# Accumulating weight-sum transfers that wait for the split of the block they follow, four steps per three blocks

## The chip, the cores and the metric

The kernel runs on one core of one Trainium2 chip. The metric is the device time of one execution in microseconds (us), median of three runs. One execution was also recorded by the hardware profiler; its rows are what the prediction argues from.

## What is computed

One layer of an encoder: a token mixer with two groups of recurrent heads, a cross-attention, and a squared-ReLU MLP, each on the RMS-normalised residual stream of 512 tokens by 1024 columns, all in float32. Cut to what matters:

```python
D_MODEL, SEQ, MEM_LEN, D_FF = 1024, 512, 256, 4096
def reference(x, mem, ...):
    x = x + token_mixer(rmsnorm(x, norm_mix[l]), w_in[l], ..., w_out[l])
    x = x + cross_attention(rmsnorm(x, norm_xattn[l]), rmsnorm(mem, norm_mem[l]), w_xq[l], w_xkv[l], w_xo[l])
    x = x + squared_relu_mlp(rmsnorm(x, norm_mlp[l]), w_up[l], w_down[l])
    return rmsnorm(x, norm_final)
def token_mixer(xn, w_in, ...):
    proj = xn @ w_in + b_in                      # q, forget gates, ... of both groups
    hgrn_out  = scan forward + scan backward     # per head, forget gate per key
    mlstm_out = scan forward + scan backward     # per head, running-max stabiliser
    return concatenate([hgrn_out, mlstm_out]) @ w_out
```

## The kernel before

All products run on TensorE as three passes of a fast float32 type: each operand is split into a high and a low part, and `mm3` (L338 to L341) multiplies high by high, high by low and low by high. The split of a weight block, `split_out` (L335, L336), is a copy to `wh` on ScalarE (ACT) and a subtraction to `wl` on VectorE (DVE); both show as L336.

Weights come as 141 blocks of 128 x 1024 (512 KB). The first 75, blocks 0 to 74, are streamed in a fixed order: the mixer's input projection (0 to 36; blocks 5 to 12 belong to the first pair of HGRN heads: q, forward gate, backward gate, output gate), cross-attention's k and v (37 to 52), the mixer's output (53 to 60), cross-attention's q (61 to 68) and the beginning of its output (69 to 74). `weights(key)` (L270) is called as each block's products are written: it splits blocks i to i+2, and has block i+3 loaded by SyncE (SP) (`load`, L251; the transfer is L256, tile `st`, three buffers, and three each of `wh` and `wl`). A load can start when the split of the block three earlier has freed its buffer.

The MLP and part of cross-attention's output use a Strassen-like scheme of seven products P1 to P7 per 2 x 2 blocks, some of which need sums of weight blocks. The DMA engines make these sums in device memory, in tiles named `form_...`: `make_forms` (L297 to L331) yields 88 steps in a fixed order. A *start* copies a block into a form (SP, L293), a *follow* copies a finished form into the next one (SP, L309), and 44 *accumulating steps* add a block into a form that its start or follow has filled (a DMA of GpSimd, POOL, with `accum_op`, L293; the name is `form_P<-in_wpk` at POOL). The first twelve steps are starts. `next_form` (L243) takes the next step: from block 6 on, `weights` calls it once per block, and twice where the block's number is divisible by four, so that 79 steps fall into the streamed blocks; the MLP's `mahead` (L1267) takes the other nine, one at every second block.

A scheduler sets the order of each engine's instructions, and a step's place in it comes from `behind` (L142): an edge without a semaphore that puts the step behind another instruction of the same engine. An SP step is placed behind the last load. An accumulating step is placed behind the last `wl` split, which is VectorE's: across engines such an edge makes nobody wait. So an accumulating step is issued as soon as GpSimd's queue comes to it and the start or follow that it adds to has landed.

GpSimd issues its instructions in order, and has other work: the pow of `rstd_of` (L209), which VectorE's L207 feeds and on which normalisations wait, memsets (`vv` L819, `t` L829 and L830), and loads of the gate and `as` blocks (L1174). `in_turn` (L198) places the pows and some memsets behind all accumulating steps taken so far but the last.

At the place that the prediction speaks of, mixer blocks 8 to 14 are multiplied while VectorE prepares the scans of both groups. Chains of small work are advanced between the blocks. The gate chain of the mLSTM heads loads a mask from memory, `rmask` (128 KB, issued by SP at L761), runs two scans for the running maximum (L775), then two with the mask (L779), then L806, L808 (ScalarE) and L809. The HGRN pair has its gates evacuated with sigmoids (ScalarE L531, L533; VectorE L535, L536) and forms products of the gates level by level (`update`, L549 to L551), which TensorE multiplies at L564. A change of the function on ScalarE brings a table load of its own.

Of the kernel before, what the change touches and what calls it, by code (L numbers as in the profile page):

```python
# [80 lines left out]
def trunk(ctx: ExitStack, tc: tile.TileContext, x, mem, wpk, vec, cst, lmask, rmask, rows, out):  # L81
# [60 lines left out]
    def behind(a, b):  # L142

        tc.add_manual_dep(a.ins, b.ins.name, mybir.DependencyInfo(mybir.DependencyClass.NoSync, mybir.DependencyReason.DATA),
                          reason="order of an engine")

    def load_x(t):
        nc.sync.dma_start(out=xtile[t], in_=x[t * P:t * P + P, :])

    row_load = nc.scalar.dma_start(out=grow1[96:97, :], in_=rows[0:1, :])  # L150
    load_x(0)
    behind(nc.scalar.dma_start(out=cs, in_=cst[:, 0:NC1]), row_load)
    for g in range(2):
# [51 lines left out]
    def rstd_of(ss, w, n):  # L205
        ms = tiny(w)
        v.tensor_scalar(out=ms, in0=ss, scalar1=1.0 / n, scalar2=EPS, op0=ALU.mult, op1=ALU.add)  # L207
        r = tiny(w)
        in_turn(gp.tensor_tensor(out=r, in0=ms, in1=nh.to_broadcast([P, w]), op=ALU.pow))  # L209
        return r, ms  # L210
# [30 lines left out]
    last_load, last_made = [None], [None]  # L241

    def next_form():  # L243

        o = next(form_steps, None)
        if o is not None:
            behind(o, last_load[0] if o.ins.engine == mybir.EngineType.SP else last_made[0])
            if o.ins.engine != mybir.EngineType.SP:
                accs.append(o)


    def load(i):
        if i >= NSTREAM or i in st_tiles:
            return
        t = T("st", 1024, 3)
        last_load[0] = nc.sync.dma_start(out=t, in_=wpk[i])  # L256
        st_tiles[i] = t

    def split(i):
        if i >= NSTREAM or i in hl_tiles:  # L260
            return
        load(i)
        s = st_tiles[i]
        hi, lo = T("wh", 1024, 3, F32R), T("wl", 1024, 3, F32R)
        made = split_out(hi, lo, s)
        last_made[0] = made[1]
        hl_tiles[i] = (hi, lo)
        return made[1]

    def weights(key):  # L270
        i = SIDX[key]
        with (tc.high_priority() if i > 2 else ExitStack()):
            for n in range(i, i + 3):
                split(n)
            load(i + 3)
        for _ in range((i >= 6) + (i >= 6 and i % 4 == 0)):
            next_form()
        return hl_tiles[i]

# [72 lines left out]
    def proj_d(mat, c0, xs, n=512, count=2):  # L352

        for j in range(count):
            wh, wl = weights(("d", mat, 0, c0 + P * j))
            ps = mmb()
            for k in range(8):
                z = slice(k * P, k * P + P)
                mm3(ps[:, :n], wh[:, z], wl[:, z], xs[k][0], xs[k][1], k == 0, k == 7)
                if k == 3:  # L360
                    tick()
            yield ps
            tick()

    def proj_t(mat, k0, c0, xs, ntile=4, pre=None, late=False):

        acc = [mmb() for _ in range(ntile)]

        def part(t, q, w):
            for k in range(2):  # L370
                kk = 2 * q + k
                xh, xl = xs[kk][0][:, t * P:t * P + P], xs[kk][1][:, t * P:t * P + P]
                z = slice(k * 512, k * 512 + 512)
                mm3(acc[t], xh, xl, w[0][:, z], w[1][:, z], kk == 0, kk == 7)

        for q in range(2 if late else 3):
            w = weights(("t", mat, k0 + 2 * q, c0))
            for t in range(ntile):
                part(t, q, w)
                if t % 2 == 1:  # L380
                    tick()
        if pre is not None:
            pre()
        tail = [(q, weights(("t", mat, k0 + 2 * q, c0))) for q in range(2 if late else 3, 4)]
        for t in range(ntile):
            for q, w in tail:
                part(t, q, w)
            yield t, acc[t]
            if t % 2 == 1:
                tick()  # L390
# [3 lines left out]
    xs = xk(xT)  # L394
    load(0)
    load_x(1)
    load(1)
    load_x(2)
    load_x(3)
    load(2)  # L400
# [577 lines left out]
    for t in range(2):  # L978
        a = mt[t]
# [7 lines left out]
        r, _ = rstd_of(ss, 1, D)  # L987
# [279 lines left out]
    def mahead(n):  # L1267
        with tc.high_priority():
            for m in range(n, n + 3):
                msplit(m)  # L1270
            for m in range(n + 3, n + 7):
                mload(m)
        if n % 2 and n >= len(JOBS):
            next_form()
        return mhl[n]
# [468 lines left out]
```

## Time and profile before

| | |
|---|---|
| Median of 3 runs | 834.73 us (832.35 to 836.01) |
| The profiled execution | 835.44 us |
| Its span, first to last instruction | 833.7 us |
| Granted clock of TensorE, mean | 0.992 |
| TensorE (PE) busy | 806.5 us, 97% |
| VectorE (DVE) busy | 618.6 us, 74% |
| ScalarE (ACT) busy | 486.0 us, 58% |
| GpSimd (POOL) busy | 95.1 us, 11% |
| DMA queue q1 (SP's), of 16 engines | 126.04 MB, 42.6% |
| DMA queue q0 (GpSimd's), of 16 engines | 39.85 MB, 26.2% |

A row of the timeline gives start, duration, engine, line, operation, output and inputs, and in brackets the time that the engine stood idle before it with what released it. A row of the chain of waits gives start, duration and what was running in the chain of work that ended last. A row of windows gives a stretch, its length, the busy time and number of instructions of PE, weight loads, DVE, ACT and POOL, then the granted clock (1.00 is full speed), the share of the DMA engines' time in use and GB/s. The numbers L... are lines of the kernel before.

### The profile page before, as it was taken

Reading aid. Unit: us, or ns where it says so; the run is one execution under the profiler, and the core shown is the slowest. Engines: PE = TensorE matmul, PEld = TensorE weight load, DVE = VectorE, ACT = ScalarE, POOL = GpSimd, SP = SyncE. Lnnn points to the kernel's source line nnn. Section 1 sums busy time; section 2 is a strip of 40 time slices with the busy share of each in tenths; the row PEclk is TensorE's granted clock in tenths of the full one; section 3 lists DMA queues with packets and bytes.
Section 4 is the critical chain, followed back from the end, with each engine's and each line's share of the span. In section 5 each row is a group of like instructions: output and inputs, shape, how many; then the busy total and the mean of one; then the engine's idle time right before and its main releaser. Section 6 shows DMA issues by size and latency. Waiting matters only on the chain.

```text
span 833.7 us, 14061 instructions
## 1 busy us (share of the span) xinstructions
PE 806.5 (97%) x5438; PEld 694.7 (83%) x5438; DVE 618.6 (74%) x1033; ACT 486.0 (58%) x854; POOL 95.1 (11%) x130
## 2 busy tenths in 40 slices
PE   8999799999999999999999999999999999999995
PEld 6787588887888988887888889988998899889974
DVE  6566786599568988655567879997479658875885
ACT  5244556444578476454455578874486458546854
POOL 2011000210042020231020012011101000100001
PEclk9999899999999999999999999999999999999998
DMA  7379822397187978997792456679976686768552
GB/s 275 117 208 279 263 92 76 110 241 246 51 229 241 263 203 303 293 222 192 227 214 65 101 127 180 213 192 313 331 236 153 227 278 202 180 203 255 172 151 101
DMA packets 56597, 167.26 MB, mean 201 GB/s; under 512 B 5393, under 2 KB 5521, under 8 KB 56530
## 3 DMA queue, kind: packets, MB, share of 16 engines
q1 hardware_dynamic: 41200, 126.04, 42.6%
q0 software_dynamic: 15040, 39.85, 26.2%
q8 instruction: 43, 0.70, 0.3%
q10 hardware_dynamic: 290, 0.47, 0.2%
q14 instruction: 24, 0.20, 0.1%
HBM read 164.24 MB, written 48.23 MB: 255 GB/s over the span
## 4 chain that ended last, share of the span: by engine, by line
PE 64%; DVE 11%; DMA 9%; issue 8%; ACT 5%; POOL 2%; POOLq 0%; ACTq 0%; SPq 0%; DVEq 0%
PE mm L339 8%; PE mm L341 8%; PE mm L340 8%; DMA st<-in_wpk 5%; PE sm L1300 4%; DVE wl L336 4%; PE sm L1298 4%; PE sm L1299 4%; PE sm L1582 3%; PE sm L1583 3%; PE sm L1581 3%; PE mm L1582 2%; PE mm L1583 2%; PE mm L1581 2%; ACT wh L336 2%
## 5 line engine op out<-in xcount | busy, mean ns | idle before, releaser
L336 DVE TENSOR_TENSOR wl<-st,wh 128x1024 fp32r<-128x1024 f32 x165 | 201.7, 1224 | 106.5 <-ACT wh L336 105.3
L336 ACT ACTIVATE wh<-st 128x1024 fp32r<-128x1024 f32 x165 | 174.2, 1057 | 169.1 <-PE mm L340 44.7
L339 PE MATMUL mm<-xT,wh 128*128 128x512 f32 x288 | 116.3, 405 | 0.0
L341 PE MATMUL mm<-xT,wl 128*128 128x512 f32 x288 | 113.6, 394 | 0.1
L340 PE MATMUL mm<-xT,wh 128*128 128x512 f32 x288 | 113.3, 393 | 0.3 <-DVE xT L1053 0.3
L1300 PE MATMUL sm<-wh,a 128*128 128x512 f32 x180 | 70.5, 392 | 1.5 <-DVE a L336 1.5
L1298 PE MATMUL sm<-wh,a 128*128 128x512 f32 x180 | 70.2, 390 | 0.9 <-DVE vv L1511 0.9
L1299 PE MATMUL sm<-wl,a 128*128 128x512 f32 x180 | 70.1, 389 | 0.0
L341 PEld LDWEIGHTS mm<-xT,wl 128*128 128x128 f32 x288 | 54.3, 189 | 12.0 <-DVE wl L336 0.3
L340 PEld LDWEIGHTS mm<-xT,wh 128*128 128x128 f32 x288 | 54.6, 190 | 11.0 <-DVE xT L1053 0.9
L339 PEld LDWEIGHTS mm<-xT,wh 128*128 128x128 f32 x288 | 54.5, 189 | 11.0 <-ACT wh L336 0.3
L293 POOL DMA_DIRECT2D form_P<-in_wpk x44 | 45.6, 1437 | 95.3 <-DMA form_P<-in_wpk 70.3
L293 POOL DMA_DIRECT2D as<-in_wpk x20 | 17.7, 934 | 255.6 <-DVE wl L336 167.5
L1300 PEld LDWEIGHTS sm<-wh,a 128*128 128x128 f32 x180 | 33.8, 188 | 9.9 <-DVE a L336 3.1
L1298 PEld LDWEIGHTS sm<-wh,a 128*128 128x128 f32 x180 | 33.8, 188 | 8.2 <-ACT wh L336 1.3
L1299 PEld LDWEIGHTS sm<-wl,a 128*128 128x128 f32 x180 | 33.8, 188 | 7.0
L1583 PE MATMUL sm<-yT,wl 128*128 128x256 f32 x128 | 36.4, 285 | 0.8 <-DVE wl L336 0.7
L336 ACT ACTIVATE wh<-as 128x1024 fp32r<-128x1024 f32 x24 | 25.4, 1058 | 20.2 <-PE sm L1300 10.7
L1582 PE MATMUL sm<-yT,wh 128*128 128x256 f32 x128 | 36.3, 284 | 0.7 <-DVE yT L336 0.7
L1582 PE MATMUL sm<-xT,wh 128*128 128x256 f32 x128 | 36.4, 285 | 0.3 <-DVE xT L336 0.2
L1582 PE MATMUL mm<-xT,wh 128*128 128x256 f32 x128 | 36.3, 284 | 0.2 <-DVE xT L336 0.2
L1583 PE MATMUL sm<-xT,wl 128*128 128x256 f32 x128 | 36.4, 285 | 0.0
(388 smaller groups left out, 2121.2 us busy)
## 6 DMA issues: line engine op xcount, KB each, us to landing
st<-in_wpk SPq DMA_DIRECT2D x123, 512.0 KB, 4.9
form_P<-in_wpk POOLq DMA_DIRECT2D x44, 512.0 KB, 10.3
st<-form_P SPq DMA_DIRECT2D x42, 512.0 KB, 5.4
form_P<-in_wpk SPq DMA_DIRECT2D x26, 512.0 KB, 8.6
as<-in_wpk POOLq DMA_DIRECT2D x24, 512.0 KB, 6.7
form_P<-form_P SPq DMA_DIRECT2D x18, 512.0 KB, 8.2
gate<-in_wpk POOLq DMA_DIRECT2D x8, 512.0 KB, 5.5
as<-form_P SPq DMA_DIRECT2D x8, 512.0 KB, 6.7
```

The source lines that it names most:

```text
L293: return eng.dma_start(out=dst, in_=mblock(st, g, *b), max_dma_last_dim=4096, **kw)
L336: return sc.activation(dst_hi, src, AF.Copy), v.tensor_tensor(out=dst_lo, in0=src, in1=dst_hi.bitcast(F32), op=ALU.subtract)
L339: pe.matmul(ps, lhsT=ah, rhs=bh, start=first, stop=False)
L340: pe.matmul(ps, lhsT=ah, rhs=bl, start=False, stop=False)
L341: pe.matmul(ps, lhsT=al, rhs=bh, start=False, stop=last)
L1298: pe.matmul(ps, lhsT=ah, rhs=bh, start=new, stop=False, **fl)
L1299: pe.matmul(ps, lhsT=ah, rhs=bl, start=False, stop=False, **fl)
L1300: pe.matmul(ps, lhsT=al, rhs=bh, start=False, stop=end and k == 1, **fl)
L1581: pe.matmul(o, lhsT=hi[:, z], rhs=xh[:, m], start=new, stop=False, **fl)
L1582: pe.matmul(o, lhsT=hi[:, z], rhs=xl[:, m], start=False, stop=False, **fl)
L1583: pe.matmul(o, lhsT=lo[:, z], rhs=xh[:, m], start=False, stop=kt == 3, **fl)
```

## The change

A second kind of edge is added, `after`, which makes the step wait by semaphore for the other instruction. Accumulating steps now use it towards the last `wl` split; the steps of SP are placed as before. And a second step is taken at blocks divisible by three, no longer at those divisible by four.

```diff
+    def after(a, b):
+        tc.add_manual_dep(a.ins, b.ins.name, mybir.DependencyInfo(mybir.DependencyClass.Sync, mybir.DependencyReason.DATA),
+                          reason="not earlier")
...
         o = next(form_steps, None)
         if o is not None:
-            behind(o, last_load[0] if o.ins.engine == mybir.EngineType.SP else last_made[0])
-            if o.ins.engine != mybir.EngineType.SP:
+            if o.ins.engine == mybir.EngineType.SP:
+                behind(o, last_load[0])
+            else:
+                after(o, last_made[0])
                 accs.append(o)
...
-        for _ in range((i >= 6) + (i >= 6 and i % 4 == 0)):
+        for _ in range((i >= 6) + (i >= 6 and i % 3 == 0)):
             next_form()
```

The last split at block i is that of block i+2. The first accumulating step was taken at block 16 and is now taken at block 15; it waits for the split of block 17. 84 of the 88 steps fall into the streamed blocks, and four accumulating steps are left to the MLP. New lines push the numbers after L145 up by five, and those after L250 by seven.

What this does to the order of GpSimd's instructions is shown from the end of its set-up to the first accumulating steps, before:

```order
L819 MEMSET vv_2094 128x4
L819 MEMSET vv_2103 128x4
L819 MEMSET vv_2157 128x4
L819 MEMSET vv_2166 128x4
L750 MEMSET a_92_579 128x512
L765 MEMSET a_98_614 64x512
L766 MEMSET a_98_614 64x512
L293 DMA form_P_0_472<-in_wpk 256x1x512 [waits DMAHW4_49]
L293 DMA form_P_0_480<-in_wpk 128x1024 [waits DMAHW7_49]
L293 DMA form_P_0_488<-in_wpk 256x1x512 [waits DMAHW0_49]
L293 DMA form_P_1_476<-in_wpk 256x1x512 [waits DMAHW2_49]
```

and now, in the same place:

```order
L757 MEMSET a_92_580 128x512
L772 MEMSET a_98_614 64x512
L773 MEMSET a_98_614 64x512
L300 DMA form_P_0_472<-in_wpk 256x1x512 [waits DMAHW4_49,DVE_49]
L300 DMA form_P_0_480<-in_wpk 128x1024 [waits DMAHW5_49]
L300 DMA form_P_0_488<-in_wpk 256x1x512 [waits DMAHW0_49,DVE_49]
L300 DMA form_P_1_476<-in_wpk 256x1x512 [waits DMAHW2_49,DVE_49]
```

Each DMA waits for the start that it adds to (DMAHW) and now for VectorE as well, where the instruction ahead of it has not waited for the same split already. The four `vv` memsets have moved behind the twelfth accumulating step, and the first pow (L209, now L214) stands behind the tenth and no longer behind the eighth.

On VectorE the order moves around the scans of the mask; `wl_640` is the split of block 11. Before:

```order
L775 SCALAR_TENSOR_TENSOR a_98_614<-a_64_391 4x512
L336 TENSOR_TENSOR wl_640<-st_597,wh_639 128x1024 [waits DMAHW6_49,PE_49,Activation_49]
L535 TENSOR_SCALAR a_99_631<-a_99_631,misc 128x512 [waits Activation_49]
L536 TENSOR_SCALAR a_100_632<-a_100_632,misc 128x512 [waits Activation_49]
L779 SCALAR_TENSOR_TENSOR a_98_614<-a_92_579,a_64_391 4x512 [waits DMAHW5_49]
L779 SCALAR_TENSOR_TENSOR a_98_614<-a_92_579,a_64_391 4x512
```

and now:

```order
L782 SCALAR_TENSOR_TENSOR a_98_614<-a_64_391 4x512
L786 SCALAR_TENSOR_TENSOR a_98_614<-a_92_580,a_64_391 4x512 [waits DMAHW5_49]
L343 TENSOR_TENSOR wl_640<-st_598,wh_639 128x1024 [waits DMAHW7_49,PE_49,Activation_49]
L542 TENSOR_SCALAR a_99_631<-a_99_631,misc 128x512 [waits Activation_49]
L543 TENSOR_SCALAR a_100_632<-a_100_632,misc 128x512 [waits Activation_49]
L786 SCALAR_TENSOR_TENSOR a_98_614<-a_92_580,a_64_391 4x512
```

The first of the two mask scans, which waits for `rmask` to land, has moved ahead of the split and of the two operations behind it. On SP the second start moves ahead of two loads; as before, five starts stand ahead of `rmask`.

## Prediction

> **What bounds the kernel now.** First the page: its span and its busy shares.
>
> ```profile
> span 833.7 us, 14061 instructions
> PE 806.5 (97%) x5438; PEld 694.7 (83%) x5438; DVE 618.6 (74%) x1033; ACT 486.0 (58%) x854; POOL 95.1 (11%) x130
> ```
>
> TensorE is busy for 806.5 of 833.7 us, so only some 27 us of idling, and whatever a slow clock stretches, can be won. The page's slices of the span show one place inside the program with both a gap and a lower clock, from 83 to 104 us. Next came the table of windows around it (columns: window, length, busy time with counts of PE, PEld, DVE, ACT, POOL, then granted clock, DMA share, GB/s), and TensorE's timeline.
>
> ```profile
> 63.00:84.00 21.00, 19.01 (x87) 15.14 (x85) 12.84 (x24) 10.44 (x15) 2.90 (x3) 1.00 1.08 280
> 84.00:105.00 21.00, 15.90 (x242) 12.72 (x243) 16.82 (x27) 11.18 (x17) 1.86 (x2) 0.84 0.87 262
> 105.00:126.00 21.00, 21.00 (x274) 16.86 (x273) 16.75 (x30) 11.98 (x20) 0.00 (x0) 1.00 0.26 81
> 86.60:90.30 3.70, 1.21 (x64) 1.07 (x64) 3.70 (x6) 2.28 (x4) 0.83 (x1) 0.50 1.09 211
> ```
>
> ```profile
> 81.40 0.39 PE L340 MATMUL mm<-xT,wh 128*128 128x512 f32 x1
> 81.63 0.39 PE L341 MATMUL mm<-xT,wl 128*128 128x512 f32 x1
> 86.65 0.66 PE L564 MATMUL sm<-t,as 128*32 128x32 f32 x32 [4.64 <-DVE as L551]
> 89.75 0.66 PE L564 MATMUL sm<-t,t 128*32 128x32 f32 x32 [2.44 <-DVE t L551]
> 90.34 0.80 PE L339 MATMUL mm<-xT,wh 128*128 128x512 f32 x1
> 93.39 0.39 PE L340 MATMUL mm<-xT,wh 128*128 128x512 f32 x1
> 94.64 0.55 PE L564 MATMUL sm<-a,as 128*32 128x32 f32 x32
> 94.99 0.22 PE L564 MATMUL sm<-a,t 128*32 128x32 f32 x2
> ```
>
> TensorE stands 4.64 us, then 2.44 us, for the two products of L551, and the clock granted in between is 0.50. The chain of waits, in order of time, says why L551 is late, and VectorE's timeline shows the wait inside it.
>
> ```profile
> 60.95 13.35 DMA a<-in_rmask
> 74.33 1.21 DVE a L779
> ...
> 79.72 1.28 ACT L531
> 81.72 1.28 ACT L804
> 83.28 1.28 ACT L533
> 89.01 0.70 DVE t L551
> ```
>
> ```profile
> 63.83 2.44 DVE L775 TENSOR_TENSOR_SCAN a<-a 4x512 f32<-4x512 f32 x2 [2.11 <-ACT a L759]
> 66.30 1.23 DVE L336 TENSOR_TENSOR wl<-st,wh 128x1024 fp32r<-128x1024 f32 x1
> 67.90 0.48 DVE L536 TENSOR_SCALAR a<-a,misc 128x512 f32<-128x512 f32 x1
> 74.33 2.44 DVE L779 TENSOR_TENSOR_SCAN a<-a,a 4x512 f32<-4x512 f32 x2 [5.95 <-DMA a<-in_rmask]
> 85.81 0.69 DVE L551 TENSOR_TENSOR as<-a 128x512 f32<-128x512 f32 x1
> ```
>
> The 128 KB load of rmask takes 13.35 us to land, VectorE stands 5.95 us for it, and everything from the scans through three table loads on ScalarE to L551 follows without slack. So what bounds this place is a transfer, in a stretch whose DMA share is 1.08. GpSimd's timeline and the DMA queues of the window 40 to 110 us (columns: packets, MB, share of 16 engines), with the issues there, say what else was in flight.
>
> ```profile
> 51.98 1.21 POOL L293 DMA_DIRECT2D form_P<-in_wpk  x1 [36.18 <-DMA form_P<-in_wpk]
> 88.74 0.83 POOL L293 DMA_DIRECT2D form_P<-in_wpk  x1 [3.59 <-DMA form_P<-in_wpk]
> 156.45 1.04 POOL L209 TENSOR_TENSOR tiny<-tiny,misc 128x4 f32<-128x4 f32 x1 [66.89 <-DVE tiny L207]
> ```
>
> ```profile
> q1 hardware_dynamic: 4498, 12.48, 50.7%
> q0 software_dynamic: 1792, 4.19, 32.9%
> form_P<-in_wpk POOLq DMA_DIRECT2D x8, 512.0 KB, 10.3
> ```
>
> Eight accumulating steps are issued from 51.98 to 88.74 us and fill 32.9% of 70 us, 23.0 us or 2.9 us each; q1 has 35.5 us for 12.48 MB, 1.49 us per 512 KB.
>
> **The change part by part.** *The wait.* The first two steps now wait for the split of block 17, whose wl L336 ends at 113.4 us here and, with the gain below, near 106. So no accumulating step runs from 52 to about 106 us. That leaves q1 to itself while rmask is under way. Between 50.5 and 60.95 us SP has issued two loads, four starts and a third load ahead of rmask: 7 x 1.49 + 0.37 = 10.8 us of queue work in 10.5 us, so almost no backlog. When the queue is quiet, the two kinds of transfer take
>
> ```profile
> st<-in_wpk SPq DMA_DIRECT2D x9, 512.0 KB, 3.5
> form_P<-in_wpk SPq DMA_DIRECT2D x2, 512.0 KB, 6.0
> ```
>
> (the loads in the window 100 to 160 us, the starts in the window 44 to 51 us). I bound rmask's landing by these two: 60.95 + 3.5 = 64.4 to 60.95 + 6.0 = 67.0, against 74.31.
>
> *Order on VectorE.* One rmask scan now stands ahead of the split of block 11 and its two TENSOR_SCALARs. The L775 scans end at 66.27, so the first scan starts at 66.3 to 67.0; the scan (1.22), split to L536 (66.30 to 68.38, 2.08) and the second scan (1.22) follow: 70.8 to 71.5 against 76.77. The second scan is 5.3 to 6.0 us earlier.
>
> *What is late next.* The chain after it shifts as a whole. The first L531 reads the sums of block 9, two blocks ahead of block 11, which TensorE ends at 81.63 + 0.39 = 82.0; a block is 24 matmuls at 0.23 (81.40 to 81.63), 5.5 us, so they have been there since about 71. The split of block 12, which stands ahead of it on ScalarE, reads a load that SP issues right before rmask. L551 ends at 86.50 - 5.3 to 6.0 = 80.5 to 81.2, before TensorE is through at 82.0: the wait of 4.64 is gone. The second L551 ends at 89.71 less as much, 83.7 to 84.4; TensorE, which needs some 0.35 us for 32 of L564 at the full clock (94.64 to 94.99), gets there at 82.4 to 82.7, and waits 1.0 to 2.0.
>
> *The clock.* From 82.0 to 93.4 TensorE does 64 of L564 and seven 512-column matmuls. At the full clock that is 2 x 0.35 + 7 x 0.23 = 2.3 us, so 9.1 us are lost there, 7.1 of them in waits and 2.0 to the clock. With only 1.0 to 2.0 us left of the waits the clock should not fall. The Trainium skill, "TensorE: Matmul & The Clock Gate", Part 1, has the clock halved after an idle window of about 3.4 us; the trace agrees as far as it goes, 0.50 after 4.64 us. Gain here: 9.1 - 1.0 to 2.0 = 7.1 to 8.1; I take 7.7.
>
> *Where the steps go.* The steps moved out run from 106 us on, where the DMA share is 0.26 and TensorE idles for nothing: free; if that cover were gone, a step costs 2.9 us of DMA time. From 168 on they come at one to two per block. The waiting steps block GpSimd's queue: behind them stand four vv memsets, the pow of L209, the gate and as loads. The first pow waits for VectorE until 156.45; ten steps (the last behind block 23, whose split ends at 152.8) are issued before. In the later stages a pow stands behind one step at most 0.3 us (block 53's split ends at 337.1, the pow was released at 338.15). I take 0; bounds 0 to 1.
>
> *Four steps per three blocks.* 84 steps instead of 79 fall in the streamed blocks, and SP's starts and copies stand earlier in front of loads. A start costs 0.5 to 0.7 us of SP's time, which waits anyway. The stage to watch is cross-attention's k and v.
>
> ```profile
> 265.00:300.00 35.00, 34.03 (x268) 32.51 (x267) 31.44 (x83) 20.46 (x50) 5.99 (x8) 1.00 0.75 211
> 300.00:336.00 36.00, 34.91 (x223) 30.25 (x222) 30.72 (x77) 24.21 (x63) 2.93 (x3) 1.00 0.89 283
> 266.67 3.99 POOL L293 DMA_DIRECT2D form_P<-in_wpk  x4 [0.39 <-issue]
> 286.30 1.06 ACT L336 ACTIVATE wh<-st 128x1024 fp32r<-128x1024 f32 x1 [1.87 <-DMA st<-in_wpk]
> 570.00:615.00 45.00, 44.00 (x306) 40.80 (x304) 26.68 (x29) 24.37 (x31) 5.99 (x6) 1.00 1.02 306
> ```
>
> TensorE loses 2.1 us in 71 there. Four steps that are issued in a burst at 266.67 spread over the splits of blocks 39 to 42 (273 to 289 us), which relieves one load and presses on another: -1 to +3, taken as 0. In the MLP the five steps fewer fall before 615 us, where 1.0 us is lost: 0 to -0.5, taken as 0.
>
> Sum: 835.44 (of which 833.7 span) - 7.7 = 827.7 for the profiled execution. That one lies 0.7 above the median, so 834.73 - 7.7 = **827.0**; by the bounds 834.73 - 8.1 - 1 - 0.5 = 825.1 to 834.73 - 7.1 + 3 + 1 = 831.6.
>
> **The rivals.**
>
> *Slower: loads of the k and v stage arrive late.* There blocks take 3.6 to 4 us and are loaded three ahead, so a load must land within some 10 us; now steps come with each split, two with every third. If the eight loads from 273 to 300 us took 13.4 us, as rmask did beside accumulating steps, against the 8.92 of the load that the chain of waits shows there,
>
> ```profile
> 277.27 8.92 DMA st<-in_wpk
> ```
>
> each would be some 4.4 us late, and with three in flight 8 / 3 x 4.4 = 11.7 us would be lost, with the clock's 2 on top: 827.0 + 13.7 = 840.7. It decides once a load takes over 10 us. For it: 286.30 already waits for its load. Against it: starts, which filled q1 at 60 us, are absent from 273 to 300. The Trainium skill, "DMA: Bandwidth & Descriptors", Queues, rings and completion order, has each DMA engine take turns between the queues by packets, whoever issued them; 13.35 against 3.5 us agrees, and by that rule moved steps press wherever they land. Chance 0.08.
>
> *Half the gain: a later wait or the clock.* If rmask lands at 69.7, between the two bounds and the 74.31 of now, the second scan ends at 69.7 + 1.22 + 2.08 + 1.22 = 74.2, 2.5 us earlier; of the first wait 4.64 - 2.5 = 2.1 stays, of the second 2.4, and half of the clock's 2.0: 9.1 - 5.5 = 3.6, or 831.1. The same comes out if k and v give back 4. Chance 0.16.
>
> *Given back.* From 168 to 213 us VectorE is busy for 43.98 of 45 us,
>
> ```profile
> 168.00:213.00 45.00, 44.50 (x566) 34.64 (x564) 43.98 (x74) 22.45 (x36) 4.03 (x8) 1.00 0.81 221
> ```
>
> so what TensorE gains earlier could be lost there to waiting for VectorE. Against it: VectorE itself is early by as much, since its own stall for rmask is what goes. Time 834.7. Chance 0.07.
>
> *rmask is late anyway*, since starts and loads alone fill the queue. The change would then not do what it is there for, and the scan ahead of block 11's split delays that split: 74.33 + 1.22 + 1.23 = 76.8, so L535, L536 and the second scan end some 2.1 us later, all of it on the chain: 836.8. Decides if rmask lands after 74. Chance 0.05.
>
> **How the numbers follow.** Forecast 0.64, half the gain 0.16, given back 0.07, rmask late 0.05, slower 0.08. Half a per cent, about what a measurement of this kernel can tell from no change, is 4.2 us: bounds 830.6 and 838.9. The forecast's own bounds, 825.1 to 831.6, are nearly all faster (0.63 of 0.64); of half the gain about half is. So faster 0.71, same 0.21 (0.08 of half the gain, given back, rmask late and a rest of the forecast), slower 0.08. The range: 824.0 (some 1 us more of the k, v and MLP waits gone) to 833.0, which takes in half the gain and leaves out the last three cases, 0.20.
>
> **What would show it.** Right: no accumulating step between 50 and 100 us; rmask lands by 67; TensorE's wait for the first L551 is gone, that for the second 1 to 2 us; granted clock 1.00 from 84 to 105. Wrong: rmask after 70; clock 0.50 after 82 us; more waits of wh L336 for st than now between 265 and 336 us; a pow of L209 that waits for GpSimd's queue. Over 833 or under 824 the sum is wrong.

## The result and the profile after

The changed kernel takes 827.61 us (median of 6 runs, 827.11 to 829.71) against 836.37 us (median of 6, 832.35 to 838.33) of the kernel before. The ratio, here and below, is taken over all the runs and is not the quotient of the medians (0.9895 here): it is 0.9904, 95% interval 0.9878 to 0.9931. The forecast was 827.0. The page of the changed kernel's profiled execution gives the span and TensorE's share:

```profile
span 826.9 us, 14074 instructions
PE 804.2 (97%) x5438; PEld 692.9 (84%) x5438; DVE 618.8 (75%) x1033; ACT 485.7 (59%) x854; POOL 96.4 (12%) x130
```

The span is 6.8 us shorter. The two windows that showed the gap before now read:

```profile
63.00:84.00 21.00, 19.70 (x151) 15.82 (x150) 17.81 (x32) 15.20 (x21) 0.00 (x0) 1.00 0.63 206
84.00:105.00 21.00, 21.00 (x273) 16.73 (x273) 18.39 (x30) 10.32 (x15) 0.00 (x0) 1.00 0.39 127
```

TensorE is busy throughout the second one, at a granted clock of 1.00 instead of 0.84, GpSimd does nothing, and the DMA share is 0.39 instead of 0.87. VectorE's timeline, with line numbers higher by seven, shows the wait for rmask gone:

```profile
63.47 2.44 DVE L782 TENSOR_TENSOR_SCAN a<-a 4x512 f32<-4x512 f32 x2 [2.11 <-ACT a L766]
65.94 1.21 DVE L786 TENSOR_TENSOR_SCAN a<-a,a 4x512 f32<-4x512 f32 x1
69.14 1.21 DVE L786 TENSOR_TENSOR_SCAN a<-a,a 4x512 f32<-4x512 f32 x1
79.40 0.69 DVE L558 TENSOR_TENSOR as<-a 128x512 f32<-128x512 f32 x1
```

The first scan with the mask follows the L782 scans without a gap, and the first L558 (L551 before) ends at 80.09. On TensorE's timeline the first of the two waits has disappeared and the second is 1.30 us; the matmuls behind it keep the full pace:

```profile
81.26 0.39 PE L348 MATMUL mm<-xT,wl 128*128 128x512 f32 x1
81.58 0.46 PE L571 MATMUL sm<-t,as 128*32 128x32 f32 x32
83.34 0.46 PE L571 MATMUL sm<-t,t 128*32 128x32 f32 x32 [1.30 <-DVE t L558]
84.07 0.39 PE L347 MATMUL mm<-xT,wh 128*128 128x512 f32 x1
```

What released all this is on the DMA side: the issues of SP in the window 53 to 70 us (the last number is us to landing), and GpSimd's first accumulating step, which waited for the split of block 17.

```profile
form_P<-in_wpk SPq DMA_DIRECT2D x5, 512.0 KB, 6.2
st<-in_wpk SPq DMA_DIRECT2D x3, 512.0 KB, 4.2
a<-in_rmask SPq DMA_DIRECT2D x1, 128.0 KB, 3.8
```

```profile
105.76 2.09 POOL L300 DMA_DIRECT2D form_P<-in_wpk  x2 [90.35 <-DVE wl L343]
```

To see where time goes in all kernels, the table further down uses one measure: every kernel issues the same 5438 matmuls, here numbered from 0 in the order in which they start. The time from the start of number 300 to that of 600, and on to 2200, 2600, 3200, 4200 and the last one, gives six stages that can be set side by side.

### The profile page after: what moved, and what is told of

It reads as the page before. It is cut to its first block, busy times and chain, and to the rows that moved or that the text cites. A ratio compares the mean times of both kernels' runs of the same rounds, so it can differ in the third digit from the quotient of the medians.

```text
span 826.9 us, 14074 instructions
## 1 busy us (share of the span) xinstructions
PE 804.2 (97%) x5438; PEld 692.9 (84%) x5438; DVE 618.8 (75%) x1033; ACT 485.7 (59%) x854; POOL 96.4 (12%) x130
## 4 chain that ended last, share of the span: by engine, by line
PE 77%; DVE 9%; issue 4%; DMA 4%; ACT 4%; POOL 1%; POOLq 0%; ACTq 0%; DVEq 0%
PE mm L346 11%; PE mm L347 11%; PE mm L348 11%; PE sm L1307 4%; PE sm L1306 4%; PE sm L1305 4%; PE sm L1589 4%; PE sm L1590 4%; PE sm L1588 4%; DVE wl L343 3%; PE mm L1589 3%; PE mm L1590 3%; PE mm L1588 3%; DMA st<-in_wpk 3%; ACT wh L343 2%
## 5 line engine op out<-in xcount | busy, mean ns | idle before, releaser
L343 ACT ACTIVATE wh<-st 128x1024 fp32r<-128x1024 f32 x165 | 174.1, 1057 | 171.9 <-PE mm L347 44.1
L1589 PE MATMUL sm<-yT,wh 128*128 128x256 f32 x128 | 36.3, 284 | 0.7 <-DVE yT L343 0.7
L1589 PE MATMUL sm<-xT,wh 128*128 128x256 f32 x128 | 36.4, 285 | 0.3 <-DVE xT L343 0.2
L1589 PE MATMUL mm<-xT,wh 128*128 128x256 f32 x128 | 36.3, 284 | 0.2 <-DVE xT L343 0.2
L1588 PE MATMUL sm<-xT,wh 128*128 128x256 f32 x128 | 36.4, 284 | 0.0
L1588 PE MATMUL mm<-xT,wh 128*128 128x256 f32 x128 | 36.3, 284 | 0.0
```

What stands on the lines that cost most here:

```text
L343: return sc.activation(dst_hi, src, AF.Copy), v.tensor_tensor(out=dst_lo, in0=src, in1=dst_hi.bitcast(F32), op=ALU.subtract)
L1588: pe.matmul(o, lhsT=hi[:, z], rhs=xh[:, m], start=new, stop=False, **fl)
L1589: pe.matmul(o, lhsT=hi[:, z], rhs=xl[:, m], start=False, stop=False, **fl)
```

## The experiments

The theory after the result: the eight accumulating steps that ran from 52 to 89 us made rmask late, and holding them back is the gain; the rest of the change is worth nothing either way. The rivals: the rate of four steps per three blocks brings a part; all transfers there were slow and rmask only the first to be seen; the later waits matter too. The first four kernels take these apart.

**The wait alone.**

```diff
-        for _ in range((i >= 6) + (i >= 6 and i % 3 == 0)):
+        for _ in range((i >= 6) + (i >= 6 and i % 4 == 0)):
```

> The wait alone, with the old rate (a second step at blocks divisible by four). Theory (accumulating steps held back from 52 to 106 us let rmask land some 10 us earlier, and that is the gain): rmask lands within 5 us of its issue, TensorE's wait for the first L558 is gone, the granted clock stays 1.00, and the time is 8 us less than before, ratio 0.990 to 0.992. Since the two scans of the mask stand together behind the split of block 11 as before, they end at about 71, as in the changed kernel. Rival (the four steps per three blocks bring a part of the gain, through fewer steps in the MLP): 3 us or more slower than the changed kernel, ratio 0.994 or more.

Measured: 838.27 us against 834.75, ratio 1.0042 (1.0030 to 1.0054). The wait alone makes the kernel slower, where 0.990 to 0.992 was expected. At 82 us it does what the theory says: the stage from matmul 300 to 600 takes 28.5 us, as in the changed kernel. The loss is in two later stages, each by about as much: k and v take 64.8 us where the kernel before took 59.6, and the stage with the MLP's first part takes 165.2 where it took 160.1. The windows of the k and v stage:

```profile
265.00:300.00 35.00, 33.69 (x267) 32.11 (x266) 31.07 (x83) 17.89 (x45) 7.97 (x8) 1.00 0.81 210
300.00:336.00 36.00, 32.12 (x184) 28.00 (x183) 25.59 (x67) 20.66 (x55) 0.87 (x1) 0.91 0.89 288
```

ScalarE's timeline names the reason in this stage, the splits of blocks 48, 49 and 50 standing for their loads one after the other, and TensorE's timeline the price:

```profile
302.26 1.06 ACT L343 ACTIVATE wh<-st 128x1024 fp32r<-128x1024 f32 x1 [4.25 <-DMA st<-in_wpk]
307.92 1.06 ACT L343 ACTIVATE wh<-st 128x1024 fp32r<-128x1024 f32 x1 [1.70 <-DMA st<-in_wpk]
310.61 1.06 ACT L343 ACTIVATE wh<-st 128x1024 fp32r<-128x1024 f32 x1 [1.34 <-DMA st<-in_wpk]
```

```profile
313.06 1.12 PE L878 MATMUL sm<-cs,yT 128*128 128x128 f32 x4 [3.80 <-ACT as L872]
```

GpSimd's rows of this kernel and of the changed one tell one thing that is different. The wait alone issues three accumulating steps just as those three loads are issued:

```profile
288.81 1.02 POOL L300 DMA_DIRECT2D form_P<-in_wpk  x1 [7.29 <-DVE t L924]
293.07 0.87 POOL L300 DMA_DIRECT2D form_P<-in_wpk  x1 [2.17 <-DVE tiny L921]
296.66 1.05 POOL L300 DMA_DIRECT2D form_P<-in_wpk  x1 [2.72 <-DVE tiny L212]
```

The changed kernel, which is further on in its list of steps, issues none from 282 to 309:

```profile
281.37 1.03 POOL L300 DMA_DIRECT2D form_P<-in_wpk  x1 [2.77 <-DVE tiny L919]
309.55 0.87 POOL L300 DMA_DIRECT2D form_P<-in_wpk  x1 [14.28 <-DVE wl L343]
```

So the theory that the rate is worth nothing falls. What the MLP's part of the loss comes from, these rows do not say.

**The rate alone.** The kernel before with `i % 3` for `i % 4`.

> Four steps per three blocks, without the wait. Theory: accumulating steps run from 52 us on as before, rmask lands at about 74, and the first mask scan, which this rate places ahead of the split of block 11, makes the second scan end 2.1 us later than before, so TensorE's wait for the first L551 is about 6.7 us and the time 1 to 3 us above before, ratio 1.000 to 1.004. Rival (the rate brings a part of the gain): ratio 0.997 or less.

Measured: 842.0 us, ratio 1.0084 (1.0070 to 1.0098), slower than the theory gave. VectorE's timeline shows the first mask scan ahead of the split of block 11, waiting, and the second one behind it:

```profile
72.86 1.21 DVE L779 TENSOR_TENSOR_SCAN a<-a,a 4x512 f32<-4x512 f32 x1 [6.91 <-DMA a<-in_rmask]
74.00 1.19 DVE L336 TENSOR_TENSOR wl<-st,wh 128x1024 fp32r<-128x1024 f32 x1
76.06 1.22 DVE L779 TENSOR_TENSOR_SCAN a<-a,a 4x512 f32<-4x512 f32 x1
```

rmask landed 1.5 us earlier than before, yet the second scan ends at 77.28 instead of 76.77: from the first scan's start it takes 4.42 us where the two together took 2.44. TensorE's first wait grew from 4.64 to 5.46 us. This is the forecast's rival "rmask is late anyway" in a kernel of its own: its price of 2.1 us for the order of the scans shows as 4.42 - 2.44 = 2.0. The stage costs 37.6 us against 36.1; 1.5 more are lost in the k and v stage and 2.9 in the MLP.

**Only rmask, earlier.** The kernel before, with the load of rmask issued one step of its chain earlier, at 30.36 us in place of 60.95; no step is held back.

```diff
+        lp = A4()
+        rm = lp[:, 512:1024]
+        nc.sync.dma_start(out=rm[0:64, 0:512], in_=rmask)
         tri = A4()
...
-        lp = A4()
...
-        rm = lp[:, 512:1024]
-        nc.sync.dma_start(out=rm[0:64, 0:512], in_=rmask)
```

> The kernel before, with nothing changed in the steps: only rmask's load is issued one step of its chain earlier, before the accumulating steps begin, so it lands before 50 us. Theory (the one late transfer is what bounds the place): VectorE's wait of 5.95 us for rmask is gone although all other transfers stay as slow as before, the scans end before 70, and TensorE's two waits shrink from 7.1 to between 0 and 2.5 us; the time is 6 to 9 us less than before, ratio 0.989 to 0.993. Rival (all loads of this stretch are slow beside accumulating steps, rmask is only the first to be seen): the split of block 12, whose load takes over 13 us, or that of block 13 takes rmask's place, and the gain is under 4 us, ratio 0.995 or more.

Measured: 826.09 us, ratio 0.9893 (0.9878 to 0.9907), as the theory of the one late transfer gave. The window of before reads, in this kernel:

```profile
63.00:84.00 21.00, 21.00 (x158) 16.94 (x157) 16.50 (x32) 13.06 (x20) 2.90 (x3) 1.00 1.07 284
```

and the transfers issued from 53 to 70 us land as late as they did before (10.4, 15.2 and 11.2 us, in the order of these rows):

```profile
form_P<-in_wpk POOLq DMA_DIRECT2D x4, 512.0 KB, 10.9
form_P<-in_wpk SPq DMA_DIRECT2D x4, 512.0 KB, 15.5
st<-in_wpk SPq DMA_DIRECT2D x3, 512.0 KB, 11.5
```

The DMA share is 1.07 as before, loads take 11.5 us, and TensorE is busy for 21.00 of 21.00 us. So slow loads cost nothing at this place; rmask alone did. What bounded it was one transfer of 128 KB that was issued when it was nearly needed.

**Only the first eight steps wait.** The changed kernel, with

```diff
-                after(o, last_made[0])
+                (after if made_accs[0] < 8 else behind)(o, last_made[0])
+                made_accs[0] += 1
```

> The changed kernel, but only the first eight accumulating steps wait; the other 36 are placed without a wait as before. Theory (only the steps that ran beside rmask matter): the time of the changed kernel within 1 us, ratio 0.989 to 0.992. Rival (spreading the later steps is a part of the gain): 2 us or more slower than the changed kernel, ratio 0.993 or more. Second rival (the later waits cost something, as the 0.85 us that the changed kernel loses again between 304 and 389 us suggest): 1 us or more faster, ratio under 0.989.

Measured: 834.26 us, ratio 0.9990 (0.9981 to 1.0000), as the first rival has it. At 82 us the gain is all there (28.5 us); but k and v take 4.4 us more than in the changed kernel and the MLP's first part 3.1 more. The later waits are a part of the result, by keeping these two stages as they were.

So the place at 82 us was as forecast, and two later stages decide the sign. A new theory for the first of them, k and v: what counts there is which steps stand beside the loads of blocks 48 to 50, and that follows from how many are done when the stage begins at block 37. Four kernels for it.

**The first eight do not wait, the others do.** The line of the last kernel with `>= 8` for `< 8`.

> The changed kernel, but the first eight accumulating steps do not wait, the other 36 do. Theory now (two places: at 82 us the first eight steps make rmask late; between 300 and 320 us loads of the k and v stage arrive late in some kernels, and there the later waits together with four steps per three blocks keep them in time): the first place is as in the kernel with the rate alone, 10 us worse than in the changed kernel, the second as in the changed kernel, so about 837, ratio 1.000 to 1.004, and TensorE has no wait over 2 us between 300 and 320. Rival (the late loads there come from the first steps' place in the queue or from chance, not from the later waits): 841 or more, ratio 1.006 or more.

Measured: 836.43 us, ratio 1.0017 (1.0003 to 1.0031). Stage 300 to 600 takes 36.3 us as before the change, k and v 60.5 us as in the changed kernel, and the longest wait of TensorE there is 1.33 us. Forecast 837.

**Four per three only up to block 36, or only from block 37 on.**

```diff
+        for _ in range((i >= 6) + (i >= 6 and i % (3 if i < 37 else 4) == 0)):
```

and the same with 3 and 4 exchanged.

> The changed kernel, but four steps per three blocks only up to block 36, then five per four as before. Theory (it matters how many steps are done when the k and v stage begins at block 37: then the starts of the second lane and the steps stand beside other loads): the time of the changed kernel within 1.5 us, ratio 0.988 to 0.992. Rival (it is the rate inside the stage): 834 or more, ratio 0.997 or more.

> The changed kernel, but five steps per four blocks up to block 36, and four per three from block 37 on. Theory (it matters how many steps are done when the k and v stage begins): as the kernel with the wait alone in that stage, a wait of TensorE of 3 us or more between 300 and 320 and a granted clock under 0.97 from 265 to 336, 834 to 840, ratio 0.998 or more. Rival (it is the rate inside the stage): the changed kernel's time within 1.5 us, ratio 0.988 to 0.992.

Measured: up to block 36, 825.96 us, ratio 0.9901 (0.9880 to 0.9922), the changed kernel's; from block 37 on, 835.12 us, ratio 1.0010 (0.9996 to 1.0024). In the latter TensorE stands 5.61 us at L878 and the k and v stage takes 67.4 us against 58.2. So in kernels where every accumulating step waits, the rate up to block 36 decides about this stage, and not the rate inside it. The two rates differ there by three steps: blocks 6 to 36 take 31 + 11 = 42 at four per three and 31 + 8 = 39 at five per four. The number alone is not enough: the kernel in which only the first eight wait has taken 42 as well, and its stage is 4.4 us longer.

**No steps beside those loads.** The slow kernel with the wait alone, with no step at blocks 43 to 47 and six more at 53 to 58:

```diff
+        for _ in range(0 if 43 <= i < 48 else (i >= 6) + (i >= 6 and i % 4 == 0) + (53 <= i < 59)):
```

> The kernel with the wait alone (five steps per four blocks), but no step is taken at blocks 43 to 47, whose loads are those of blocks 46 to 50; six more are taken at blocks 53 to 58 in return. Theory (the steps taken at those blocks make the loads of blocks 48 to 50 land late, and that is where the wait alone gives its gain back): those loads land within 7 us, TensorE's wait of 3.8 us at L878 is gone, the granted clock is 1.00 from 265 to 336, and the time is 4 to 7 us less than with the wait alone, 830 to 834, ratio 0.994 to 0.998. Rival (that stage's loads are late through the stage's own traffic, or the time is lost in the MLP): 836 or more, ratio 1.001 or more.

Measured: 831.89 us (829.12 to 836.59), ratio 0.9958 (0.9936 to 0.9981): 6.4 us less than with the wait alone. The loads issued from 288 to 306 us, of the wait alone (first) and with the steps held back (second), and the window:

```profile
st<-in_wpk SPq DMA_DIRECT2D x5, 512.0 KB, 9.4
form_P<-in_wpk POOLq DMA_DIRECT2D x3, 512.0 KB, 10.3
```

```profile
st<-in_wpk SPq DMA_DIRECT2D x5, 512.0 KB, 4.2
form_P<-in_wpk POOLq DMA_DIRECT2D x1, 512.0 KB, 8.0
```

```profile
300.00:336.00 36.00, 35.92 (x212) 31.12 (x211) 29.74 (x81) 25.91 (x70) 3.99 (x4) 1.00 0.85 256
```

The loads are back at 4.2 us, TensorE is busy for 35.92 of 36 us at the full clock, and the stage takes 59.0 instead of 64.8 us. This shows that in the kernel with the wait alone the steps taken at these blocks caused the late loads. The MLP's first part stays slow (165.9 us), so about half of what the wait alone loses has another cause.

**Versions that might beat both.** With rmask early as above, on the changed kernel; the same with four per three up to block 36; the changed kernel with `i % 2`, so that all 88 steps fall into the streamed blocks; and `i % 2` with rmask early.

> The changed kernel, with rmask's load issued one step of its chain earlier as well. Theory (what is left at 82 us is 1.3 us of waiting behind the mask scans, which end earlier when rmask does not have to be waited for): 0 to 2 us faster than the changed kernel, ratio 0.987 to 0.991, TensorE's wait at L571 gone. Rival (the two gains add, because each removes something of its own, the late mask and the slow loads): 5 us or more faster than the changed kernel, ratio 0.984 or less.

> The changed kernel with rmask's load one step of its chain earlier and four steps per three blocks only up to block 36, five per four after. Theory (the two places are independent): 82 us as in the kernel with both, k and v as in the kernel with the rate up to block 36, so 824 to 827 and the lowest of all, ratio 0.986 to 0.990. Rival (what is left is shifted by each of these from one late load to another): the changed kernel's time or more, ratio 0.990 or more.

> The changed kernel with three steps per two blocks, so that all 88 steps fall into the streamed blocks and the second lane's starts come before block 37. Theory (the more is done before k and v, the better for that stage, until the steps fill the queue ahead of rmask or stand closer than one per 2.9 us of DMA time): rmask still lands within 8 us, k and v lose no more than in the changed kernel, 824 to 830, ratio 0.987 to 0.994. Rival (a denser row of steps only moves the late loads to an earlier stage): a wait of 2 us or more for a split before 265 us, or a clock under 0.98 somewhere before it, 832 or more, ratio 0.996 or more.

> Three steps per two blocks with the wait, and rmask's load one step of its chain earlier. Theory (the places are independent: 82 us without any wait, no steps left for the MLP): 1 to 2 us under the kernel with three steps per two blocks, 824 to 826, ratio 0.985 to 0.988, the lowest of all. Rival (what is taken away at one place comes back at the next late load): 826.5 or more, ratio 0.988 or more.

Measured, in this order: 827.06 us, ratio 0.9905 (0.9882 to 0.9929); 826.0, ratio 0.9891 (0.9870 to 0.9912); 826.53, ratio 0.9882 (0.9862 to 0.9902); 823.75, ratio 0.9859 (0.9834 to 0.9884). The wait for L571 is gone wherever rmask is early, the gains of the wait and of the early rmask do not add, and `i % 2` does not delay rmask (4.5 us to landing). It does make a load late, that of block 43: ScalarE stands 2.65 us for it at 280.57, but the stage takes 60.0 us, no more than in the changed kernel. The last of the four is the fastest kernel of all, though its interval still touches the changed kernel's (0.9878 to 0.9931); among the other three and the changed kernel no order can be told. The page of the last:

```profile
span 821.2 us, 14074 instructions
PE 803.9 (98%) x5438; PEld 693.7 (84%) x5438; DVE 618.4 (75%) x1033; ACT 483.0 (59%) x852; POOL 94.6 (12%) x130
```

The stages of all, in us, from one profiled execution each, and the ratio. Runs of one kernel spread by 2 to 7.5 us, so a small difference between two rows tells nothing. In the kernel before the stages run from 68 to 104 us, the place of the gap, then to 278, to 337 (k and v), to 459, to 619 (the MLP's first part among it) and to the end.

| kernel | 300 to 600 | to 2200 | to 2600 | to 3200 | to 4200 | to last | ratio |
|---|---|---|---|---|---|---|---|
| before | 36.1 | 173.5 | 59.6 | 121.4 | 160.1 | 205.7 | 1 |
| changed | 28.5 | 174.1 | 60.2 | 121.4 | 160.0 | 205.9 | 0.9904 |
| wait alone | 28.5 | 173.5 | 64.8 | 121.3 | 165.2 | 206.3 | 1.0042 |
| rate alone | 37.6 | 173.8 | 61.1 | 121.4 | 163.0 | 204.5 | 1.0084 |
| rmask early | 27.0 | 173.4 | 59.7 | 121.7 | 160.1 | 206.8 | 0.9893 |
| first 8 wait | 28.5 | 173.8 | 64.6 | 121.4 | 163.1 | 204.6 | 0.9990 |
| others wait | 36.3 | 174.0 | 60.5 | 121.4 | 162.0 | 205.0 | 1.0017 |
| 4 per 3 to block 36 | 28.5 | 173.9 | 58.2 | 121.4 | 161.3 | 205.5 | 0.9901 |
| 4 per 3 from block 37 | 28.5 | 173.9 | 67.4 | 121.7 | 160.2 | 204.6 | 1.0010 |
| wait, held at 43 to 47 | 28.5 | 173.5 | 59.0 | 122.1 | 165.9 | 205.4 | 0.9958 |
| changed, rmask early | 27.0 | 173.9 | 59.6 | 121.6 | 161.2 | 205.9 | 0.9905 |
| 4 per 3 to block 36, rmask early | 27.0 | 173.9 | 58.2 | 121.7 | 161.6 | 204.8 | 0.9891 |
| 3 per 2 | 28.4 | 173.9 | 60.0 | 121.4 | 158.1 | 204.3 | 0.9882 |
| 3 per 2, rmask early | 27.0 | 174.0 | 59.0 | 121.7 | 158.1 | 204.7 | 0.9859 |

Three columns hold nearly all differences: the place at 82 us, k and v, and the MLP's first part.

## Why the prediction was right, and where its working was not

**rmask's landing and the scans.** Expected at 64.4 to 67.0, landed 3.84 us after its issue at 60.60, 64.4. The second scan was put at 70.8 to 71.5 and ends at 69.14 + 1.21 = 70.35. That is under the range because everything here runs 0.35 us earlier, the issue of rmask (60.60 for 60.95) too. One reading was off by a block, without effect: the load issued right before rmask, at 60.57, is that of block 13. Block 12's was issued at 53.97 and landed 10.4 us later, long before its split at 78.66.

**The two waits and the clock.** The first L551 was put at 80.5 to 81.2 and ends at 80.09; the second wait at 1.0 to 2.0 us and is 1.30; the clock was to stay at 1.00 and does. That waits of 1 to 2 us leave the clock alone is no rule, though: another kernel shows it fall after one of 2.00 us (last section). The place was worth 7.1 to 8.1 with 7.7 taken; the stage shrinks by 36.1 - 28.5 = 7.6. That this gain hangs on rmask alone is shown by the kernel that moves only its load and gains 9.1 in the same stage.

**The order on VectorE.** The scan ahead of the split of block 11 was costed at nothing, because rmask would be in time, and with a price of 2.1 if not. Both hold: the wait alone, which keeps the old order, has the same 28.5 us; the rate alone pays 2.0 us.

**Waits in GpSimd's queue.** Taken as 0, bounds 0 to 1. From 300 to 2200 matmuls were spaced as before but for 0.6 us, so this is about right; no run separates it from other causes.

**Four steps per three blocks, taken as 0.** As a number for this change it holds: k and v take 0.6 us more, the MLP 0.1 less. As a step of the argument it does not. The working summed the wait and the rate as if they were independent, and allowed k and v 3 us at most. With the wait, the rate is worth 838.27 - 827.61 = 10.7 us (by the ratios 1.0042 - 0.9904 = 1.4%), 4.6 of it in k and v and 5.2 in the MLP's first part; without it, it costs 842.0 - 834.75 = 7.3 us. The forecast came out right because the change has both parts, and in this it was lucky. A reader who had taken the wait alone from the same working would have forecast 827 for a kernel that takes 838.

**The rival of late loads in k and v** named that mechanism and gave it 0.08. It is real, but its price and its condition were off. It costs 5.0 to 7.8 us of stage time (64.6 to 67.4 less 59.6), not 13.7, and a load of over 10 us does not decide it. In the changed kernel two loads issued from 280 to 290 us, of blocks 46 and 47, take 13.4 us in the median, and ScalarE stands for both:

```profile
295.28 1.06 ACT L343 ACTIVATE wh<-st 128x1024 fp32r<-128x1024 f32 x1 [1.37 <-DMA st<-in_wpk]
300.46 1.06 ACT L343 ACTIVATE wh<-st 128x1024 fp32r<-128x1024 f32 x1 [3.33 <-DMA st<-in_wpk]
```

So ScalarE stands longer for loads than before between 265 and 336 us (4.7 against 2.9 us), much as in one of the prediction's own signs of being wrong. Yet TensorE loses only 1.52 us for it, at L878, and the stage takes 0.6 us more. In the kernel before, the splits of blocks 47, 49 and 50 read:

```profile
306.21 1.06 ACT L336 ACTIVATE wh<-st 128x1024 fp32r<-128x1024 f32 x1 [2.85 <-issue]
313.05 1.06 ACT L336 ACTIVATE wh<-st 128x1024 fp32r<-128x1024 f32 x1 [0.65 <-DMA st<-in_wpk]
318.06 1.06 ACT L336 ACTIVATE wh<-st 128x1024 fp32r<-128x1024 f32 x1 [0.38 <-DMA st<-in_wpk]
```

The load of block 47, issued at 295.09, landed there in 3.5 us, 7.6 us ahead of its split. In the changed kernel it takes 12.8 us, 9.3 more, so only some 1.7 us exceed the slack. The loads of blocks 49 and 50 had no slack: ScalarE stood for them already. In the kernel with the wait alone the load of block 49 takes 11.4 us where it took 8.2, and TensorE stands 3.80 us. So what decides, by these sums, is whether a late load belongs to a block without slack; no kernel tests that by itself. The forecast counted loads and steps in the stage, and should have gone through the blocks one by one. Its reason against the rival did not carry over either: that starts are absent from 273 to 300 us holds for the kernel before but for one at 295.47, while the changed kernel issues seven there, from 277.89 on.

The Trainium skill, "DMA: Bandwidth & Descriptors", Issuing engines are not separate DMA queues, says that transfers issued by ScalarE, SyncE and GpSimd run on the same DMA engines and interleave. The held-back kernel fits that: with two accumulating steps and six starts fewer beside them, the loads take 4.2 instead of 9.4 us.

**What stays open.** In the stage with the MLP's first part the kernels take from 158.1 to 165.9 us. Having no steps left there goes with the shortest stage, in two kernels, but no run tells which steps or loads cost the time in the others. A part of it is the clock: in the five kernels that take 162.0 us or more (the wait alone, the rate alone, the first 8, the others, and the one with steps held back) the granted clock is 0.98 from 545 to 615 us, in the others 1.00. Nor was it tried which of the held-back steps, the accumulating ones or the starts, made the loads late. And the medians of before and after lie 8.8 us apart where the profiled executions lie 6.8 apart; runs of before alone spread over 6 us.

## What to carry to other kernels

Look first for the one transfer on which a stall hangs, and ask whether it can be issued earlier: moving one small load gained as much as the whole change (0.9893 against 0.9904), and every other stage stayed within 1.1 us of what it was. A wait that moves transfers out of one place puts them beside other loads; go through those block by block, with the slack that each has, since the same edit can gain or lose some 10 us by which loads it meets. And a term that is zero for a whole change can be two large ones that cancel.

## What the runs showed of the hardware

The clock granted to TensorE can fall within a wait of 3.07 us. The kernel in which only the first eight steps wait shows the wait on TensorE's timeline, and the clock in the windows around its end:

```profile
315.85 1.66 PE L895 MATMUL sm<-vv,as 128*128 128x129 f32 x6 [3.07 <-ACT as L874]
312.00:316.00 4.00, 0.93 (x5) 0.45 (x3) 1.99 (x3) 3.19 (x10) 0.00 (x0) 0.85 1.04 386
316.00:318.00 2.00, 2.00 (x8) 1.91 (x9) 2.00 (x7) 0.71 (x5) 0.00 (x0) 0.50 1.06 367
```

TensorE stands from 312.78 to 315.85. A mean clock of 0.85 over the 4 us up to 316, with 0.50 at their end, comes out if it fell 1.2 us before 316 (an estimate from these rows), some 2.0 us into the wait. In the kernel with the wait alone, the clock is 0.50 shortly after a wait of 2.00 us:

```profile
603.41 0.39 PE L1588 MATMUL sm<-yT,wh 128*128 128x256 f32 x1 [2.00 <-ACT rg L1608]
605.00:607.00 2.00, 2.00 (x12) 2.00 (x11) 0.28 (x1) 1.37 (x2) 0.00 (x0) 0.50 1.03 244
```

After one of 2.23 us it stayed up, in the kernel with rmask early and four per three up to block 36:

```profile
568.02 0.50 PE L1305 MATMUL sm<-wh,a 128*128 128x512 f32 x1 [2.23 <-ACT wh L343]
545.00:615.00 70.00, 67.01 (x443) 61.39 (x441) 48.18 (x56) 40.09 (x53) 8.60 (x9) 1.00 0.95 262
```

So in these runs the length of a single wait does not tell whether the clock falls. The Trainium skill, "TensorE: Matmul & The Clock Gate", Part 1, speaks of an idle window of about 3.4 us that is free-running, so that it need not begin with a wait. The falls after some 2.0 us are short of that length, and no run here shows where such a window begins.
